# Row factors of the five block boundaries: sums of squares by a matrix of ones, root and reciprocal on 128x320

## The chip, the cores and the metric

The kernel runs on one core of a Trainium2 chip. What counts is the device time of one execution in microseconds, as the median of several runs. The profile is of one execution by itself, with its own time.

## The reference

A recurrent decoder trunk of two layers is computed in f32 for 320 tokens (256 of a new sequence, 64 of eight short continuations), with a model width of 1024:

```python
for l in range(DEPTH):                                   # 2
    h = swiglu(rmsnorm(x, ffn1_norm_pre[l]), ffn1_w_up[l], ffn1_w_down[l])
    x = x + 0.5 * rmsnorm(h, ffn1_norm_post[l])
    h, cb, rh, S = mixer(rmsnorm(x, mix_norm_pre[l]), ...)
    x = x + rmsnorm(h, mix_norm_post[l])
    h = swiglu(rmsnorm(x, ffn2_norm_pre[l]), ffn2_w_up[l], ffn2_w_down[l])
    x = x + 0.5 * rmsnorm(h, ffn2_norm_post[l])
y = rmsnorm(x, final_norm)

def rmsnorm(x, g):
    return x * rsqrt(mean(x * x, axis=-1, keepdims=True) + EPS) * g
```

The mixer has an input projection, a short convolution, a gated linear recurrence, a gated delta rule in chunks and an output projection. Outputs are y and the states.

## The kernel before

Everything is held with channels on the 128 partitions and the 320 tokens along the row: x is eight tiles of 128x320 (k = 0 to 7), and so is hp, the output of the block that just ended. Each weight tile of 128x1024 comes by DMA (`raw`), is rounded on ScalarE (`wh`, L129), and its remainder is taken on VectorE (`wl`, L134). Activations are split in the same way into `xh` and `xl`. A weight unit is then 24 products on TensorE (L157): eight channels by wh with xh, wl with xh, wh with xl, each with 320 columns.

The stream of such units is a `Fill` object `F`: `F(n)` issues the next n products, `F.inter(4, 1)` one channel step of four units at once (12 products), `F.warm(12)` twelve dummy products that keep TensorE going. TensorE's order is the order in which the code is written; the other engines' order is made by a scheduler from priorities, and `tc.high_priority` moves an instruction ahead. Accumulators are PSUM tiles in three rings: mm (3), sm (4) and st (1).

Between two blocks stands `boundary` (L402). There are five: into the mixer (first and fourth, near 235 and 859 us of the span), into the second feed-forward block (second and fifth, near 416 and 1041 us) and into the next layer's first one (third, near 638 us). Each needs two factors per token, that is two times a sum of squares over 1024 channels, a root and a reciprocal:

- The first factor scales hp before it is added to x. The squares of the block's output are added up on VectorE in `acc`, but for the last tile (`slast`). `sumsq_mm` (L228) multiplies slices of 128 tokens by one column of ones, so that the sums lie with tokens on partitions (128x3). `rstd` (L233) takes root (L235) and reciprocal (L236) there, and `rowbc` (L239) spreads each column over a tile and transposes it on TensorE (L242), so that each token's factor lies on all partitions, in PSUM. Then for each k VectorE multiplies hp by it (`bt`, L422), adds it to x (L423), ScalarE and VectorE split x (L225, L226) and ScalarE squares it (L426), and `F.inter` runs the step of the first four units of the next block.
- The second factor is that of the next norm. It isn't applied to x but to the results of the products: it is put into `rsb2` (128x320 in SBUF, L437), and the consumers of each unit multiply by it (L496, L498 in a feed-forward block; L705, L706 for the mixer's eight scalar columns, L667, L668 for its convolution columns). `F(10)` issues ten products while root and reciprocal run.

Two tables set how many products stand between the steps. `ahead` is 8 for feed-forward blocks and 0 for mixers: so many products stand ahead of the second sums. `FL[0]` is the number of products ahead of the transposes of the mixer's scalar projection (L753 in `Mixer.run`), which wait for L705 and L706. `side` holds small work that TensorE does in a boundary: transposes of states (L601) in mixers, of outputs (L1246, L1255) in the second and fifth.

Of the kernel before, what the change touches and what calls it, by code (L numbers as in the profile page):

```python
# [11 lines left out]
AF = mybir.ActivationFunctionType  # L12
# [3 lines left out]
D = 1024  # L16
# [4 lines left out]
T = NP + NB * SL  # L21
# [34 lines left out]
PS = [(0, 1, 2), (0, 2, 1), (0, 2, 1)]  # L56
PO = [0, 0, -1, 0, 1, 1, -1, 2, 2, -1, 2, 1, -1]
XC = []
FL = [14, 37, 32, 9, 15, 8, 0, 14, 0, 11, 10, 4, 0, 11, 5, 0, 11, 12, 14, 6, 0, 11, 16]
FZ = [11, 11, 11, 22, 8, 17]  # L60
FY = [10, 10, 5, 3, 11, 6]

# [1 line left out]
def bc(ap, n):  # L64
    return ap.to_broadcast([ap.shape[0], n])
# [15 lines left out]
def trunk(ctx, tc, x_prompt, x_sample, state_conv, state_rglru, state_delta,  # L81
# [6 lines left out]
    act, dve, pe, pool = nc.scalar.activation, nc.vector, nc.tensor, nc.gpsimd  # L88
# [18 lines left out]
    def smtile():  # L107
        return smp.tile([128, 512], F32, name="sm")
# [7 lines left out]
    def sttile():  # L116
        return stp.tile([128, 512], F32, name="st")
# [87 lines left out]
    ones = consts.tile([128, 128], F32, name="ones")  # L205
    eps_t = consts.tile([128, 1], F32, name="eps_t")
    x = consts.tile([128, KD, T], F32, name="x")
    hp = consts.tile([128, KD, T], F32, name="hp")
    xh = consts.tile([128, KD, T], F32R, name="xh")
    xl = consts.tile([128, KD, T], F32R, name="xl")  # L210
    acc = consts.tile([128, T], F32, name="acc")
    rsb2 = consts.tile([128, T], F32, name="rsb2")
# [7 lines left out]
    def sqtile():  # L220
        return tmp.tile([128, T], F32, name="sq", bufs=3)

    def split_x(k, g):
        h = hv(xh[:, k])
        act(h, pr(x[:, k]), AF.Copy, scale=g)  # L225
        stt(hv(xl[:, k]), pr(x[:, k]), g, h.bitcast(F32), op0=OP.mult, op1=OP.subtract)  # L226

    def sumsq_mm(ps, s, start, stop):  # L228
        for t, (a, b) in enumerate(TOK):
            pe.matmul(ps[:, t:t + 1], s[:, a:b], ones[:, 0:1], start=start and t == 0, stop=stop,  # L230
                      skip_group_check=True)

    def rstd(ps, eps=None):  # L233
        rs = tmp.tile([128, 3], F32, name="rs")
        act(rs, ps[:, 0:3], AF.Sqrt, scale=1.0 / D, bias=eps_t if eps is None else eps)  # L235
        dve.reciprocal(rs, rs)  # L236
        return rs

    def rowbc(rs):  # L239
        rb = smtile()  # L240
        for t, (a, b) in enumerate(TOK):
            pe.transpose(rb[:, a:b], bc(rs[:, t:t + 1], 128), ident)  # L242
        return rb

    sq_first = {}

    def accum(i, n, s, eng=None):
        eng = eng or dve
        if i == 0:
            sq_first[0] = s  # L250
        elif i == 1:
            eng.tensor_add(acc, sq_first[0], s)
        elif i < n - 1:
            eng.tensor_add(acc, acc, s)
# [25 lines left out]
    def vcol(nm, i):  # L280
        return C["vec"][:, 0, rows[nm] + i:rows[nm] + i + 1]
# [119 lines left out]
    def boundary(slast, gname, l, F, n, side, ahead=0):  # L401
        side = list(side) + [None] * 3  # L402
        cnt[0] = -1
        if side[0]:
            side[0]()
        st = sttile()
        sumsq_mm(st, acc, True, False)
        sumsq_mm(st, slast, False, True)
        if side[1]:
            side[1]()  # L410
        with tc.high_priority(offset=HPB):
            rs = rstd(st)
        rb = rowbc(rs)
        if side[2]:
            side[2]()
        F.warm(12)
        st2 = sttile()
        for k in range(KD):
            if k != 1:
                t = tmp.tile([128, T], F32, name="bt")  # L420
            with tc.high_priority(offset=HPB):
                dve.tensor_mul(t, hp[:, k], rb[:, :T])  # L422
                dve.tensor_add(x[:, k], x[:, k], t)  # L423
                split_x(k, vcol(gname, 8 * l + k))
            s = sqtile()
            act(s, x[:, k], AF.Square)  # L426
            accum(k, KD, s, pool if AP else dve)
            F.inter(n, 1)
        F.i = n
        F(ahead)  # L430
        sumsq_mm(st2, acc, True, False)
        sumsq_mm(st2, s, False, True)
        with tc.high_priority(offset=HPB):
            rs = rstd(st2)
        F(10)
        rb2 = rowbc(rs)
        act(rsb2, rb2[:, :T], AF.Copy)  # L437

    def xtoken():
        z = tmp.tile([128, 1], F32, name="tk", bufs=6)  # L440
# [168 lines left out]
    class Mixer:  # L609
# [37 lines left out]
        def mt(self, shape, name, bufs=1, dt=F32):  # L647
            return self.mp.tile(shape, dt, name=name, bufs=bufs)
# [88 lines left out]
        def run(self):  # L737
# [11 lines left out]
            F.inter_done(4, 2)  # L749
            F(FL[0])  # L750
            tp = smtile()
# [32 lines left out]

            F(FL[1])
            self.late_state()
            F(FL[2])
            gp = smtile()
# [16 lines left out]
            qg = mt([128, NH, 192], "qg")  # L805
            F(FL[3])
            grs = []
# [34 lines left out]
            def tok(u0, src, srcs, dst, scl, sums=None):  # L842
                n = 4 if u0 < 8 else 2
                ps = smtile()
                for i in range(n):
                    if u0 < 8:
                        a = src[:, i, 32 * u0:32 * u0 + 128]
                    else:
                        a = srcs[:, 2 * i:2 * i + 2]
                    pe.transpose(ps[:, i * 128:(i + 1) * 128], a, ident)  # L850
                if sums is not None:
                    with tc.high_priority(offset=HPO):
                        for i in range(n):
                            act(dst[:, u0 + i], ps[:, i * 128:(i + 1) * 128], AF.Square,
                                accum_out=sums[:, u0 + i:u0 + i + 1])
                for i in range(n):
                    u = u0 + i
                    act(dst[:, u], ps[:, i * 128:(i + 1) * 128], AF.Copy, scale=scl[:, u:u + 1])
# [3 lines left out]

            F(FL[4])
            for u0 in (0, 4, 8):
                tok(u0, ka, kas, kd, eKD, ss)
                F(FL[5])
            with tc.high_priority(offset=HPO):
# [412 lines left out]
    F = ph.F  # L1280
# [117 lines left out]
    rs = rstd(ss)  # L1398
    rb2 = smtile()
# [16 lines left out]
    for l in range(DEPTH):  # L1416
        side = state_prep(l)
        mids = [(14, side[0])]
        if l == 0:
            mids = [(4 + i, consts_a) for i in range(12)] + [(18, consts_b), (22, side[0])]  # L1420
        s = ph.run(mids)
        mx = Mixer(l, side)
        boundary(s, "mpre", l, mx.F, mx.n, [None, side[2]])
        s = mx.run()
        ph = ffn2(l)
        boundary(s, "f2pre", l, ph.F, ph.n, mx.outputs(ph.fp), 8)
        if l + 1 < DEPTH:
            nxt_side = None
            s = ph.run()
            ph = ffn1(l + 1)  # L1430
            boundary(s, "f1pre", l + 1, ph.F, ph.n, [], 8)
        else:
            ph.run_last()
# [32 lines left out]
```

## Time and profile before

| | |
|---|---|
| median of 3 runs | 1289.98 us (1288.92 to 1290.28) |
| the profiled execution | 1285.95 us, span 1284.2 us |
| TensorE busy with matmuls | 1250.6 us, 97% of the span |
| TensorE busy with weight loads | 1216.2 us, 95% |
| VectorE | 854.0 us, 66% |
| ScalarE | 699.4 us, 54% |
| the chain that ended last | TensorE 89%, VectorE 4%, ScalarE 3% |
| granted clock of TensorE over the span | 0.982 |

A line of a group names the line of the code, the engine, the operation and its tiles. A matmul of f32 tiles shows as two records, a product of rounded tiles as one. Matmuls are pipelined, so that the time from one start to the next is what one costs in a stream, and not its duration.

### The profile page before, as it was taken

The numbers are of one execution on the slowest core, as the hardware profiler recorded it, in microseconds if no ns is written. First come the engines' busy times: TensorE is split into PE (matmuls) and PEld (weight loads), VectorE is DVE, ScalarE is ACT, GpSimd is POOL, SyncE is SP. The second block draws the span as 40 slices with busy tenths as digits, with TensorE's granted clock in tenths as the row PEclk, the third lists the DMA queues.
The fourth block names the chain that finished last, engine by engine and source line by source line (L and its number), as shares of the span: only waits on it lengthen the run. The fifth ranks groups of instructions, "written<-read, shape, count | busy, mean of one in ns | idle before, by whom it ended". The sixth has DMA issues, their size and how long they took to land.

```text
span 1284.2 us, 24470 instructions
## 1 busy us (share of the span) xinstructions
PE 1250.6 (97%) x9812; PEld 1216.2 (95%) x9812; DVE 854.0 (66%) x1536; ACT 699.4 (54%) x1223; POOL 111.9 (9%) x242
## 2 busy tenths in 40 slices
PE   8999999999999999999999999999998999999995
PEld 7999999989879999999999999999897899999995
DVE  4976644799686866654586665459995777666433
ACT  5654444584686644444464444446658675444443
POOL 1100000233120100000000000012321110000001
PEclk8999999999989999999999999999999899999997
DMA  8555555553346455555635555575332646555541
GB/s 211 156 172 159 156 160 161 144 144 90 94 122 177 114 162 164 165 151 162 190 108 163 164 164 152 159 194 132 83 89 70 180 142 177 161 160 155 148 136 42
DMA packets 356102, 187.26 MB, mean 146 GB/s; under 512 B 8986, under 2 KB 353388, under 8 KB 355988
## 3 DMA queue, kind: packets, MB, share of 16 engines
q1 hardware_dynamic: 352980, 178.25, 49.3%
q0 software_dynamic: 2672, 6.65, 1.9%
q8 instruction: 77, 1.26, 0.4%
q10 hardware_dynamic: 336, 0.79, 0.2%
q14 instruction: 37, 0.30, 0.1%
HBM read 179.16 MB, written 6.51 MB: 145 GB/s over the span
## 4 chain that ended last, share of the span: by engine, by line
PE 89%; DVE 4%; ACT 3%; DMA 1%; SPq 1%; issue 1%; POOL 1%; ACTq 0%; DVEq 0%
PE mm L157 43%; PE sm L157 38%; PE sm L907 2%; PE st L230 1%; PE sm L1194 1%; PE sm L971 1%; DMA xtok<-in_x_sample_dram 1%; ACT wh L129 0%; ACT hp L1072 0%; DMA raw<-in_ffn_w_up_dram 0%; DVE xr L1097 0%; ACT vo L1078 0%; POOL sv L869 0%; ACT hp L1079 0%; DVE DN L821 0%
## 5 line engine op out<-in xcount | busy, mean ns | idle before, releaser
L134 DVE TENSOR_TENSOR wl<-raw,wh 128x1024 fp32r<-128x1024 f32 x321 | 384.5, 1198 | 214.0 <-ACT wh L129 209.8
L129 ACT ACTIVATE wh<-raw 128x1024 fp32r<-128x1024 f32 (+1 forms) x316 | 326.7, 1035 | 360.4 <-issue 125.4
L157 PE MATMUL mm<-xh,wh 128*128 128x320 f32 x976 | 295.9, 307 | 1.6 <-ACT wh L1332 0.9
L157 PE MATMUL mm<-xh,wl 128*128 128x320 f32 x976 | 293.6, 305 | 0.9 <-DVE wl L134 0.9
L157 PE MATMUL mm<-xl,wh 128*128 128x320 f32 x976 | 287.4, 304 | 0.0
L157 PE MATMUL sm<-xh,wh 128*128 128x320 f32 x720 | 215.6, 299 | 0.0
L157 PE MATMUL sm<-xl,wh 128*128 128x320 f32 x720 | 215.5, 299 | 0.0
L157 PE MATMUL sm<-xh,wl 128*128 128x320 f32 x720 | 215.4, 299 | 0.0
L157 PEld LDWEIGHTS mm<-xh,wh 128*128 128x128 f32 x976 | 187.1, 193 | 7.5 <-issue 3.0
L157 PEld LDWEIGHTS mm<-xh,wl 128*128 128x128 f32 x976 | 185.9, 192 | 3.3 <-DVE wl L134 1.3
L157 PEld LDWEIGHTS mm<-xl,wh 128*128 128x128 f32 x976 | 184.3, 192 | 1.8 <-issue 0.8
L157 PEld LDWEIGHTS sm<-xh,wl 128*128 128x128 f32 x720 | 136.1, 189 | 0.3 <-DVE wl L134 0.3
L157 PEld LDWEIGHTS sm<-xh,wh 128*128 128x128 f32 x720 | 136.1, 189 | 0.0
L157 PEld LDWEIGHTS sm<-xl,wh 128*128 128x128 f32 x720 | 136.1, 189 | 0.0
L157 PE MATMUL sm<-gh,wh 128*128 128x320 f32 x374 | 112.2, 300 | 0.0
L157 PE MATMUL sm<-gh,wl 128*128 128x320 f32 x374 | 111.8, 299 | 0.0
L157 PE MATMUL sm<-gl,wh 128*128 128x320 f32 x374 | 111.8, 299 | 0.0
L157 PE MATMUL mm<-gh,wh 128*128 128x320 f32 x330 | 99.0, 300 | 0.0
L157 PE MATMUL mm<-gh,wl 128*128 128x320 f32 x330 | 98.7, 299 | 0.0
L157 PE MATMUL mm<-gl,wh 128*128 128x320 f32 x330 | 98.7, 299 | 0.0
L157 PEld LDWEIGHTS sm<-gh,wl 128*128 128x128 f32 x374 | 70.7, 189 | 0.0
L157 PEld LDWEIGHTS sm<-gh,wh 128*128 128x128 f32 x374 | 70.7, 189 | 0.0
(438 smaller groups left out, 1969.5 us busy)
## 6 DMA issues: line engine op xcount, KB each, us to landing
raw<-in_ffn_w_up_dram SPq DMA_DIRECT2D x173, 512.0 KB, 3.9
raw<-in_ffn_w_down_dram SPq DMA_DIRECT2D x64, 512.0 KB, 3.9
raw<-in_w_in_dram SPq DMA_DIRECT2D x48, 512.0 KB, 4.1
raw<-in_ffn_w_down_dram SPq DMA_DIRECT2D x32, 384.0 KB, 3.5
raw<-in_w_out_dram SPq DMA_DIRECT2D x16, 512.0 KB, 4.1
aux<-in_state_delta_dram SPq DMA_DIRECT2D x8, 512.0 KB, 7.3
out_dram<-aux POOLq DMA_DIRECT2D x8, 512.0 KB, 5.7
raw<-in_ffn_w_up_dram SPq DMA_DIRECT2D x6, 256.0 KB, 7.3
```

What stands on the lines that cost most here:

```text
L129: act(wh[:, :nk], raw[:, :nk], *((AF.Copy,) if tok is None or tok[0] else (AF.Identity, tok[1]())))
L134: (sub or dve).tensor_sub(wl[:, :nk], raw[:, :nk], wh[:, :nk].bitcast(F32))
L157: pe.matmul(self.blk.ps(), w, il(xx), start=self.first and self.pos == 1, stop=self.last and self.pos == 3 * self.nk)
L230: pe.matmul(ps[:, t:t + 1], s[:, a:b], ones[:, 0:1], start=start and t == 0, stop=stop, skip_group_check=True)
L907: pe.matmul(ps[HF[h], 64 * i:64 * i + 64], lhs(u, h), rhs(u, h), start=True, stop=True)
L971: pe.matmul(ps[32 * j:32 * j + 32, 128 * i:128 * i + 128], kz[:, h, i, c:c + 32], SS[p][:, j // 2, 4 * (j % 2) + b], start=b == 0, stop=b ...
L1194: pe.matmul(ps2[j], kd[r, u], ve[r], start=True, stop=True)
```

## The change

The sums of squares are made with the full 128x128 matrix of ones as the stationary operand and the squares (128x320) as the moving one, so that every partition of the result holds each token's sum. Root and reciprocal then work on 128x320 and write `rsb2`; the transposes go. Both factors of a boundary go through `rsb2`. The ten products ahead of the second transposes go, and `FL[0]` goes from 14 to 18.

```diff
-FL = [14, 37, 32, 9, 15, 8, 0, 14, 0, 11, 10, 4, 0, 11, 5, 0, 11, 12, 14, 6, 0, 11, 16]
+FL = [18, 37, 32, 9, 15, 8, 0, 14, 0, 11, 10, 4, 0, 11, 5, 0, 11, 12, 14, 6, 0, 11, 16]
...
+    pst = []
+
+    def sums(a, b):
+        pst[:] = [sttile()]
+        pe.matmul(pst[0][:, :T], ones, a, start=True, stop=False)
+        pe.matmul(pst[0][:, :T], ones, b, start=False, stop=True)
+
+    def rowfactor():
+        act(rsb2, pst[0][:, :T], AF.Sqrt, scale=1.0 / D, bias=eps_t)
+        dve.reciprocal(rsb2, rsb2)
...
-        st = sttile()
-        sumsq_mm(st, acc, True, False)
-        sumsq_mm(st, slast, False, True)
+        sums(acc, slast)
         if side[1]:
             side[1]()
         with tc.high_priority(offset=HPB):
-            rs = rstd(st)
-        rb = rowbc(rs)
+            rowfactor()
...
         F.warm(12)
-        st2 = sttile()
...
-                dve.tensor_mul(t, hp[:, k], rb[:, :T])
+                dve.tensor_mul(t, hp[:, k], rsb2)
...
-        sumsq_mm(st2, acc, True, False)
-        sumsq_mm(st2, s, False, True)
+        sums(acc, s)
         with tc.high_priority(offset=HPB):
-            rs = rstd(st2)
-        F(10)
-        rb2 = rowbc(rs)
-        act(rsb2, rb2[:, :T], AF.Copy)
+            rowfactor()
```

The scheduler also changes the order on VectorE. In the first boundary, behind the last weight splits of the block that ended, it was this for the first factor (numbers tell buffers apart: bt_2704 is the product of k = 0 and then of k = 1, bt_2745 that of k = 2):

```order
L236 RECIPROCAL rs_2683<-rs_2683 128x3 [waits Activation_49]
L422 TENSOR_TENSOR bt_2704<-hp_82,sm_2686 128x320 [waits PE_49]
L423 TENSOR_TENSOR x_81<-x_81,bt_2704 128x320 [waits DVE_49]
L422 TENSOR_TENSOR bt_2704<-hp_82,sm_2686 128x320 [waits DVE_49]
L422 TENSOR_TENSOR bt_2745<-hp_82,sm_2686 128x320
```

and is now this (bt_2694 is k = 0, bt_2735 is k = 2):

```order
L254 RECIPROCAL rsb2_86<-rsb2_86 128x320 [waits Activation_49]
L429 TENSOR_TENSOR bt_2694<-hp_82,rsb2_86 128x320 [waits DVE_49]
L429 TENSOR_TENSOR bt_2735<-hp_82,rsb2_86 128x320
L430 TENSOR_TENSOR x_81<-x_81,bt_2694 128x320 [waits DVE_49]
L430 TENSOR_TENSOR x_81<-x_81,bt_2735 128x320 [waits DVE_49]
L429 TENSOR_TENSOR bt_2694<-hp_82,rsb2_86 128x320 [waits DVE_49]
```

The product of k = 2 now stands ahead of the sum of k = 0. At the end of the same boundary, for the second factor, VectorE had this row (wl are remainders of weight units of the mixer, PY the scaled scalar columns, cb the convolution's input):

```order
L134 TENSOR_TENSOR wl_2876<-raw_2873,wh_2875 128x1024 [waits DMAHW1_49,Activation_49]
L619 TENSOR_TENSOR wsl_9701<-wsr_9699,wsh_9700 128x64 [waits Activation_49]
L134 TENSOR_TENSOR wl_2884<-raw_2881,wh_2883 128x1024 [waits DMAHW2_49,Activation_49]
L236 RECIPROCAL rs_2870<-rs_2870 128x3 [waits Activation_49]
L134 TENSOR_TENSOR wl_3016<-raw_3013,wh_3015 128x1024 [waits DMAHW3_49,PE_49,Activation_49]
L705 TENSOR_TENSOR PY_2903<-sm_2690,rsb2_86 8x320 [waits Activation_49]
L706 TENSOR_TENSOR PY_2903<-sm_2690,rsb2_86 8x64
L667 TENSOR_TENSOR cb_2906<-mm_2713,rsb2_86 128x256 [waits PE_49]
```

and has this:

```order
L134 TENSOR_TENSOR wl_2907<-raw_2904,wh_2906 128x1024 [waits DMAHW1_49,Activation_49]
L622 TENSOR_TENSOR wsl_9644<-wsr_9642,wsh_9643 128x64 [waits Activation_49]
L134 TENSOR_TENSOR wl_2915<-raw_2912,wh_2914 128x1024 [waits DMAHW2_49,Activation_49]
L134 TENSOR_TENSOR wl_2997<-raw_2994,wh_2996 128x1024 [waits DMAHW3_49,Activation_49]
L254 RECIPROCAL rsb2_86<-rsb2_86 128x320 [waits Activation_49]
L708 TENSOR_TENSOR PY_2859<-sm_2681,rsb2_86 8x320 [waits DVE_49,PE_49]
L709 TENSOR_TENSOR PY_2859<-sm_2681,rsb2_86 8x64
L670 TENSOR_TENSOR cb_2862<-mm_2703,rsb2_86 128x256 [waits PE_49]
```

The third remainder now stands ahead of the reciprocal, and the scaled columns follow right behind the reciprocal, without a transpose in between.

## Rows read from the trace of the kernel before

**Rows 1.** The chain that ended last, in order of time: start, us, what.
```profile
445.43 9.78 PE mm L157 x72
```

**Rows 2.** Timeline of the first boundary's first factor: start us, us, engine, line, operation.
```profile
234.81 0.44 ACT L450 ACTIVATE sq<-sm 128x320 f32<-128x320 f32 x1 [1.38 <-PE sm L157]
...
235.30 0.83 PE L230 MATMUL st<-ones,sq 128*128 128x1 f32 x6
...
236.47 0.18 DVE L236 RECIPROCAL rs<-rs 128x3 f32<-128x3 f32 x1 [1.78 <-ACT rs L235]
...
237.28 0.49 DVE L422 TENSOR_TENSOR bt<-hp,sm 128x320 f32<-128x320 f32 x1 [0.63 <-PE sm L242]
...
238.32 0.59 ACT L225 ACTIVATE xh<-x,vec 128x320 fp32r<-128x320 f32 x1 [1.30 <-DVE x L423]
...
238.97 0.30 PE L157 MATMUL sm<-xh,wsh 128*8 128x320 f32 x1
```

**Rows 3.** VectorE's groups by form: count, busy us, mean ns, idle before.
```profile
L499 DVE TENSOR_TENSOR t<-t,t 128x320 f32<-128x320 f32 x88 | 43.2, 494 | 8.8 <-ACT t L497 1.1
...
L236 DVE RECIPROCAL rs<-rs 128x3 f32<-128x3 f32 x12 | 2.1, 175 | 19.3 <-ACT rs L235 19.1
L766 DVE RECIPROCAL sv<-sv 128x10 f32<-128x10 f32 x2 | 0.4, 216 | 0.0
L266 DVE RECIPROCAL sp<-sp 128x10 f32<-128x10 f32 x2 | 0.4, 206 | 0.0
...
L559 DVE RECIPROCAL sq<-sq 128x1 f32<-128x1 f32 x3 | 0.4, 147 | 0.0
```

**Rows 4.** ScalarE's groups by form: an activation out of PSUM with a bias column.
```profile
L1072 ACT ACTIVATE hp<-sm,vec 128x320 f32<-128x320 f32 x16 | 7.0, 521 | 0.0
```

**Rows 5.** Timeline of the first mixer: f32 matmuls with 320 columns, ten records.
```profile
347.21 2.85 PE L1071 MATMUL sm<-xr,wbd 128*128 128x320 f32 x10
```

**Rows 6.** Timeline of the first boundary, TensorE's second and third channel step.
```profile
242.22 0.30 PE L157 MATMUL sm<-xl,wsh 128*8 128x320 f32 x1 [0.20 <-DVE xl L226]
...
242.77 0.30 PE L157 MATMUL sm<-xh,wsh 128*8 128x320 f32 x1
```

**Rows 7.** Stretches: length, busy PE, PEld, DVE, ACT, POOL, granted clock, DMA share, GB/s.
```profile
281.40:284.80 3.40, 1.02 (x16) 0.83 (x14) 2.28 (x10) 2.73 (x5) 1.50 (x4) 1.00 0.09 25
284.80:288.20 3.40, 3.40 (x20) 3.28 (x17) 3.31 (x11) 3.03 (x9) 0.00 (x0) 0.50 0.02 5
32.78:34.21 1.43, 0.00 (x0) 0.03 (x1) 1.15 (x2) 1.05 (x3) 0.00 (x0) 1.00 1.10 283
34.21:38.00 3.79, 3.79 (x27) 3.55 (x28) 2.64 (x8) 2.55 (x4) 0.78 (x2) 1.00 1.18 282
```

**Rows 8.** Timeline of the second boundary's second factor.
```profile
434.90 0.72 PE L230 MATMUL st<-ones,acc 128*128 128x1 f32 x6
...
436.16 0.38 PE L157 MATMUL sm<-xl,wh 128*128 128x320 f32 x1
...
437.60 0.49 PE L242 MATMUL sm<-ident,rs 128*128 128x128 f32 x3
...
438.07 0.30 PE L157 MATMUL sm<-xh,wl 128*128 128x320 f32 x1
...
438.65 0.49 DVE L496 TENSOR_TENSOR t<-mm,rsb 128x320 f32<-128x320 f32 x1 [0.72 <-ACT rsb L437]
...
440.26 1.22 DVE L134 TENSOR_TENSOR wl<-raw,wh 128x1024 fp32r<-128x1024 f32 x1
```

**Rows 9.** Timeline of the first boundary's second factor, ahead of the mixer.
```profile
252.55 0.72 PE L230 MATMUL st<-ones,acc 128*128 128x1 f32 x6
...
253.58 1.23 DVE L134 TENSOR_TENSOR wl<-raw,wh 128x1024 fp32r<-128x1024 f32 x1 [0.72 <-ACT wh L129]
...
256.77 0.20 DVE L706 TENSOR_TENSOR PY<-sm,rsb 8x64 f32<-8x64 f32 x1
...
257.57 0.35 PE L753 MATMUL sm<-ident,PY 8*128 8x8 f32 x3
```

## The prediction

> **What bounds the kernel now.** I read the chain of work that ended last first. In the long stretches it is TensorE alone: 72 products of the weight loops in 9.78 us [rows 1], 0.136 us each, without a gap. So an edit in VectorE or ScalarE counts only where TensorE waits for them. The change touches the five boundaries between blocks (near 235, 416, 638, 859 and 1041 us of the span), and each has two such places.
>
> The first place is the row factor of the block that just ended. In the first boundary the last square is ready at 234.81 + 0.44 = 235.25 us; then come, one behind the other, the sums on TensorE (235.30, 0.83 us), a tiny root and a 0.18 us reciprocal on 128x3 (236.47), three transposes, the first product on VectorE at 237.28, the sum, the split into xh at 238.32, and the first real product of TensorE at 238.97 [rows 2]: 3.72 us in which TensorE does only dummy products and small transposes. The second place is the factor of the next norm. There TensorE has weight products to do, so it loses only what its own queue holds: in the feed-forward boundaries from 434.90 to 436.16 for the sums and from 437.60 to 438.07 around the transposes [rows 8]. In the two mixers three transposes of the scalar projection follow at 257.57 [rows 9], and they need the factor's consumers.
>
> **The unknown: a reciprocal on 128x320.** The trace has none that wide, but it has the operation at 1, 3 and 10 elements a partition: 147, 175, 206 and (another line) 216 ns [rows 3]. It grows with width. A plain VectorE operation on 128x320 takes 494 ns [rows 3], so about 0.49 us is the lower end. The flattest of the measured slopes is (206 - 175) / 7 = 4.4 ns an element, which gives 0.175 + 317 x 4.4 ns = 1.57 us; from 1 to the dearer 10 it is (216 - 147) / 9 = 7.7 ns, which gives 2.6 us. I take 2.1 us, the middle of the two slopes, since nothing in the rows favours one of them; 0.49 to 2.6 us stay as ends.
>
> The Trainium skill (VectorE: DVE Perf Modes, First, the fixed hardware budget) says that the reciprocal runs as a hardware iterative divide with a repeat count of 8, which speaks against making it wide. With the 0.96 GHz of that page an estimate is 320 x 8 / 0.96 = 2.67 us and a start of some 0.15, together 2.8; the sum below would then be 4.9 us higher, 1309.3. The trace agrees that width costs, at a somewhat lower slope, 4.4 to 7.7 ns.
>
> **A. First factor, five times.** The sums become two f32 matmuls of 128x320. Such matmuls took 2.85 us for ten records, two to a matmul [rows 5], so 0.57 us a matmul; the one on the last square would end near 236.0 instead of 236.13, and the other is done before. The root on 128x320 out of PSUM with a bias column is like the 521 ns activation [rows 4]: 236.04 to 236.56. The reciprocal runs 236.60 to 238.70. The transposes and their two handovers go, which took 237.28 - 236.65 = 0.63 us [rows 2]. VectorE's order also moves: the product of k = 2 now stands ahead of the sum of k = 0, some 0.4 us. So product at 238.72, sum near 239.5, xh near 240.06, and 0.65 us behind it, as now, TensorE at 240.7: 1.74 us later. Of this a part comes back: now the low half of k = 1 is late and TensorE reaches k = 2 only at 242.77 [rows 6], though 24 products of 0.136 from 238.97 would end at 242.23; that 0.54 us can be caught while the start is late anyway. Between 1.20 and 1.74 I take 1.35 us, and the same for the other four, whose steps are the same: +6.8 us. Each 0.1 us of reciprocal is worth 0.5 us here.
>
> **B. The clock.** TensorE now does its dummies at once, as nothing ahead of them waits for the factor, and then stands. Sums issued by 235.85, small transposes to 236.4, twelve dummies to 238.1: an idle 2.5 us until 240.7 in mixer boundaries one and four, some 3 us in the third, which has no transposes there, and 1.5 us in the other two, where output transposes fill more. In the trace of before a stretch in which TensorE was busy for 1.02 of 3.40 us was followed by one with a granted clock of 0.50, 1.2 instead of 2.4 GHz, for 3.4 us; after an idle 1.43 us the clock stayed at 1.00 [rows 7]. So three first factors, and the two mixer stalls under D (2.6 us idle), are long enough to lose the clock. 3.4 us at half speed cost 1.7 us where TensorE is the bound, and about 1.2 us at the first factor, where it waits 0.5 us anyway: all five would be 3 x 1.2 + 2 x 1.7 = 7.0 us. Not every fall need come; I take +5.0 us, with 0 and 7 as ends.
>
> **C. Second factor, three feed-forward boundaries.** The sums took 1.26 us of TensorE (434.90 to 436.16) and take four records, 1.1 us; the transposes took 438.07 - 437.60 less one product, 0.33 us, and go [rows 8]. Together -0.5 each, -1.5 us. The wide root and reciprocal lie beside the weight products: TensorE has 64 of them, 8.7 us, before it needs an accumulator that the first consumer (438.65) frees, and the next low weight half (440.26 to 441.48) is not due until then, near 444.8; both come some 1 to 2 us later. Were the cover gone, each would cost that much.
>
> **D. Second factor, two mixers.** Here it is on the path. The three low-half splits now stand ahead of the reciprocal on VectorE: the second runs from 253.58 for 1.23 us [rows 9], the third behind it to 256.05, the reciprocal to 258.15, and the two scalar products, 0.4 and 0.2 us, to 258.8. TensorE meanwhile has only 18 products (24 and the transposes before), is done at 253.6 + 2.45 = 256.1, and waits 2.6 us for the scalar transposes: 258.82 instead of 257.57. Six products that stood ahead are still to do, 0.82 us. Together +2.05 each, +4.1 us; queued behind the reciprocal on VectorE are all convolution copies, so the chain behind it is not ahead to make this good. With a reciprocal of 0.49 us it would be +0.4 each.
>
> **The sum.** 6.8 + 5.0 - 1.5 + 4.1 = +14.4 us on the profiled execution's 1285.95 us, so 1300.4. The median of the runs, 1289.98 us, is 4.0 higher, so 1304.4.
>
> **Rivals.** (1) The cost in width is only a fill that is over after a few elements, and 128x320 costs about 0.54 us. For it: the rise from 3 to 10 is less than from 1 to 3 in ns an element. Against it: it still rises, and a plain fill would show at width 1. Then A is 1.35 - 1.56 = -0.2 each, the idle times stay under 1 us so B is 0, C stays, D is 2 x 0.5: -1.0 - 1.5 + 1.0 = -1.5 us, 1288.5, no change. The point from which it decides: seven waits on the path (five A, two D) against 1.5 us saved, break-even near 0.75 us, 1.9 ns an element. (2) The reciprocal is slow but the clock holds: B is 0, 1299.4. For it: the idle stretches are hardly longer than those that lost the clock, and 12 dummies stand right ahead. (3) VectorE becomes the bound behind the boundaries: 2.1 us more of it, where it also has the splits and the gate products of every unit, makes the next weight halves late, about 2 us at each of three feed-forward blocks: 1310.4. Against it: 3.3 us of slack at 441.48.
>
> **How the numbers follow.** Forecast 0.60, rival 1 0.10, rival 2 0.20, rival 3 0.10. Low end: reciprocal 1.57 (seven times 0.53 less, -3.7) and no fall (-5.0) is +5.7, 1295.7; high end: 2.6 (+3.5) and all falls (+2.0) is +19.9, 1309.9. The scheduler's reordering of the mixers' ScalarE and VectorE queues, unpriced, adds 2 to 3 on either side: 1293.5 to 1313. Outside lie rival 1 and some of the tails. Slower by over 0.2% (2.6 us, about what a measurement here can tell from none) holds for all but rival 1 and a tail: 0.88; within 0.2% 0.08; faster 0.04.
>
> **What would show it.** The width of the reciprocal's ten rows, 2.1 us or 0.5, decides most. The first real product should come 1.7 us later against the last square. The clock should read 0.50 right behind the boundaries. In the mixers the scalar transposes should show an idle wait on VectorE of over 2 us; in feed-forward blocks TensorE should run through. Wrong would be: reciprocals under 0.8 us, or a delay that a mixer's later waits swallow.

## The result: 1.8% slower, and the profile of the changed kernel

| | before | after |
|---|---|---|
| median of 4 runs | 1289.54 us | 1312.39 us |
| lowest and highest | 1288.92 to 1290.28 | 1311.10 to 1315.14 |
| ratio after / before | | 1.0179, 95% interval 1.0164 to 1.0194 |
| profiled execution | 1285.95 us | 1311.10 us |
| its span | 1284.2 us | 1309.4 us |

The time lies in the forecast range (1293.5 to 1313) at its upper end, 8 us above the forecast 1304.4. The sign and the price of the reciprocal were right; where the 8 us come from is the question of the experiments. The profiled run of before took 3.6 us less than the median of its runs, so what is read from the two traces adds up to 25.15 us, where the medians differ by 22.85.

VectorE's group by line, with lowest, median and highest duration in ns, answers [rows 3]:

```profile
L254 DVE RECIPROCAL rsb<-rsb x10: 2145/2150/2153, 237.0 to 1087.0; 128x320 f32<-128x320 f32 x10
```

The first boundary's first factor, by engine (start us, us, engine, line, operation, idle before and who ended it), answers [rows 2]:

```profile
234.95 0.70 PE L249 MATMUL st<-acc,ones 128*128 128x320 f32 x2
235.64 0.81 PE L250 MATMUL st<-sq,ones 128*128 128x320 f32 x2
...
236.98 1.80 PE L197 MATMUL sm<-xh,wsh 128*8 128x320 f32 x12
241.78 0.30 PE L157 MATMUL sm<-xh,wsh 128*8 128x320 f32 x1 [3.01 <-ACT xh L225]
...
236.49 0.53 ACT L253 ACTIVATE rsb<-st,eps_t 128x320 f32<-128x320 f32 x1 [0.48 <-PE st L250]
...
237.04 2.15 DVE L254 RECIPROCAL rsb<-rsb 128x320 f32<-128x320 f32 x1 [2.02 <-ACT rsb L253]
239.23 1.47 DVE L429 TENSOR_TENSOR bt<-hp,rsb 128x320 f32<-128x320 f32 x2
240.63 1.41 DVE L430 TENSOR_TENSOR x<-x,bt 128x320 f32<-128x320 f32 x2
```

Sums, root, reciprocal stand one behind the other as forecast, and TensorE stands still for 3.01 us ahead of its first real product. Two things were not forecast: the pairs on L429 and L430 take 1.47 and 1.41 us, though one such operation takes 0.49 [rows 2, 3] and a pair 0.89 in the third boundary (below), and nothing is caught up later (table below).

The second factor ahead of the first mixer, VectorE and then TensorE, answers [rows 9]:

```profile
256.42 2.36 DVE L134 TENSOR_TENSOR wl<-raw,wh 128x1024 fp32r<-128x1024 f32 x2 [0.72 <-ACT wh L129]
258.70 2.15 DVE L254 RECIPROCAL rsb<-rsb 128x320 f32<-128x320 f32 x1
...
261.53 0.32 PE L756 MATMUL sm<-ident,PY 8*128 8x8 f32 x3 [2.45 <-issue]
```

And the second factor in the second boundary, answers [rows 8]: TensorE runs through it, and VectorE's reciprocal lies beside weight products.

```profile
446.75 0.70 PE L249 MATMUL st<-acc,ones 128*128 128x320 f32 x2
...
448.82 2.15 DVE L254 RECIPROCAL rsb<-rsb 128x320 f32<-128x320 f32 x1
```

Start times of TensorE's marks in the two traces, and what each stage added (a fall of the clock is a stretch at 1.2 GHz, 3.4 us or longer in these traces; "(clock)" marks the one in this table):

| mark on TensorE | before | after | later by | added since the mark above |
|---|---|---|---|---|
| first boundary, sums | 234.61 | 234.95 | 0.34 | |
| first real product | 238.97 | 241.78 | 2.81 | +2.5 (first factor) |
| second sums | 252.55 | 255.40 | 2.85 | 0 |
| scalar transposes of the mixer | 257.57 | 261.53 | 3.96 | +1.1 (second factor) |
| second boundary, sums | 416.16 | 426.47 | 10.31 | **+6.35 (rest of the mixer)** |
| first real product | 420.69 | 432.47 | 11.78 | +1.5 |
| second sums | 434.90 | 446.75 | 11.85 | +0.1 |
| third boundary, sums | 637.61 | 648.86 | 11.25 | -0.6 (second factor, feed-forward) |
| first real product | 641.96 | 655.11 | 13.15 | +1.9 |
| second sums | 656.36 | 671.01 | 14.65 | +1.5 (clock) |
| fourth boundary, sums | 859.06 | 873.12 | 14.06 | -0.6 |
| first real product | 863.42 | 879.92 | 16.50 | +2.4 |
| scalar transposes | 882.02 | 899.61 | 17.59 | +1.1 |
| fifth boundary, sums | 1040.72 | 1064.69 | 23.97 | **+6.4** |
| first real product | 1045.24 | 1070.69 | 25.45 | +1.5 |
| end of the span | 1284.24 | 1309.39 | 25.15 | -0.3 |

Of 25 us nearly 13 arise inside the two mixers, behind the scalar transposes, in code that the change doesn't touch. It is not the clock: over these stretches, 257.57 to 416.16 and 882.02 to 1040.72 us before, 261.53 to 426.47 and 899.61 to 1064.69 after, the mean granted clock is 0.96 in all four. Where TensorE waits there is seen in its waits of over 0.8 us in the first mixer, behind the scalar transposes; before, then after:

```profile
284.57 0.54 PE L890 MATMUL sm<-ka 128*64 128x64 f32 x8 [2.38 <-DVE nA L914]
351.14 1.88 PE L1071 MATMUL sm<-xr,wbd 128*128 128x320 f32 x6 [1.08 <-ACT hp L1072]
370.27 2.07 PE L1194 MATMUL sm<-nA,kd 32*128 32x512 f32 x2 [2.14 <-DVE qa L1158]
```

```profile
288.85 2.08 PE L888 MATMUL sm<-ka 128*128 128x128 f32 x8 [3.85 <-DVE nA L917]
360.02 1.88 PE L1074 MATMUL sm<-xr,wbd 128*128 128x320 f32 x6 [2.17 <-ACT hp L1075]
380.84 2.07 PE L1197 MATMUL sm<-nA,kd 32*128 32x512 f32 x2 [3.63 <-DVE tok L725]
```

The three waits last 5.60 us before and 9.65 after, 4.05 of the 6.35; two shorter ones that before doesn't have, 0.76 and 0.52 us, are 1.3 more. The first of the three is told by ScalarE's queue, and by what it feeds. Before, then after: squares of kd, the load of an activation table, and the addition that needs all ten squares. A power on GpSimd (2.25 and 2.00 us) and then nA, which TensorE waits for, follow on it:

```profile
279.56 0.30 ACT L854 ACTIVATE kd<-sm 128x128 f32<-128x128 f32 x1
...
281.00 1.28 ACT L700 ACT_TABLE_LOAD   x1
...
279.98 0.17 DVE L868 TENSOR_SCALAR sv<-sv 128x10 f32<-128x10 f32 x1
```

```profile
282.64 1.28 ACT L703 ACT_TABLE_LOAD   x1
...
284.51 0.27 ACT L857 ACTIVATE kd<-sm 128x128 f32<-128x128 f32 x1
...
284.90 0.17 DVE L871 TENSOR_SCALAR sv<-sv 128x10 f32<-128x10 f32 x1 [1.11 <-ACT kd L857]
```

Before, the tenth square starts at 279.56 and the table load stands behind all ten. After, eight squares run, then the load of 1.28 us, an activation, and only then the last two, the tenth at 284.51. The scheduler has put ScalarE's instructions in another order. The other two waits lead back to the queues in the same way. Before, then after: what ScalarE runs ahead of the hp that the second wait ends on, and when VectorE reaches the qa that the third wait ends on:

```profile
349.40 1.28 ACT L1056 ACTIVATE qa<-qa,fs 128x128 f32<-128x128 f32 x4 [0.91 <-POOL fs L1051]
...
369.81 0.41 DVE L1158 TENSOR_TENSOR qa<-sm,kso 128x256 f32<-128x256 f32 x1
```

```profile
356.44 1.28 ACT L1081 ACT_TABLE_LOAD   x1
...
358.29 1.26 ACT L1059 ACTIVATE qa<-qa,fs 128x128 f32<-128x128 f32 x4
...
379.26 1.19 DVE L134 TENSOR_TENSOR wl<-raw,wh 128x1024 fp32r<-128x1024 f32 x1
380.38 0.41 DVE L1161 TENSOR_TENSOR qa<-sm,kso 128x256 f32<-128x256 f32 x1
```

After, a table load and one activation stand ahead of qa and hp on ScalarE (before, that load stands behind them, at 353.61), and a weight remainder stands ahead of the other qa on VectorE (before, the next one comes behind it, at 370.93). The trace names tok, which starts right behind qa, as the end of the third wait after; qa ends 0.05 us ahead of TensorE's start in both traces. Both traces have 31 table loads: none was added, they moved.

The clock behind the first and the third boundary (length, busy PE, PEld, DVE, ACT, POOL, granted clock, DMA share, GB/s), answers [rows 7]:

```profile
238.78:241.78 3.00, 0.00 (x0) 0.00 (x0) 2.96 (x5) 0.58 (x1) 2.91 (x7) 1.00 1.10 248
241.80:245.20 3.40, 3.08 (x21) 2.54 (x22) 3.40 (x9) 2.42 (x6) 0.00 (x0) 1.00 0.04 9
...
656.50:659.90 3.40, 3.40 (x15) 3.40 (x14) 3.40 (x10) 1.92 (x5) 0.00 (x0) 0.51 0.00 0
```

TensorE idled 3.00 us in the first and kept 2.4 GHz; behind the third it ran at 1.2 GHz for 3.4 us. Of the five falls that the prediction counted, three at first factors and two at the mixers' new stalls, this profile has one. (Its other falls lie inside the mixers.)

### The profile page after: what moved, and what is told of

Same layout as the page of the kernel before. It is cut to its first block, busy times and chain, and to the rows that moved or that the text cites. A ratio compares the mean times of both kernels' runs of the same rounds, so it can differ in the third digit from the quotient of the medians.

```text
span 1309.4 us, 24249 instructions
## 1 busy us (share of the span) xinstructions
PE 1247.6 (95%) x9702; PEld 1206.4 (92%) x9702; DVE 872.2 (67%) x1536; ACT 699.1 (53%) x1218; POOL 116.2 (9%) x242
## 3 DMA queue, kind: packets, MB, share of 16 engines
q8 instruction: 76, 1.25, 0.4%
## 4 chain that ended last, share of the span: by engine, by line
PE 84%; DVE 7%; ACT 5%; issue 2%; DMA 1%; POOL 0%; ACTq 0%; DVEq 0%
PE mm L157 41%; PE sm L157 36%; PE sm L910 2%; DVE wl L134 1%; DVE rsb L254 1%; ACT wh L129 1%; DMA raw<-in_ffn_w_up_dram 1%; PE sm L1197 1%; PE sm L974 1%; ACT hp L1075 1%; DVE xr L1100 0%; DVE bt L429 0%; DMA xtok<-in_x_sample_dram 0%; ACT kd L857 0%; PE st L250 0%
## 5 line engine op out<-in xcount | busy, mean ns | idle before, releaser
L157 PE MATMUL mm<-xh,wh 128*128 128x320 f32 x976 | 295.7, 308 | 6.9 <-ACT xh L225 6.8
L157 PE MATMUL mm<-xh,wl 128*128 128x320 f32 x976 | 294.1, 306 | 0.8 <-DVE wl L134 0.4
L157 PE MATMUL mm<-xl,wh 128*128 128x320 f32 x976 | 287.0, 304 | 0.0
L157 PE MATMUL sm<-xl,wh 128*128 128x320 f32 x720 | 216.0, 300 | 0.0
L157 PE MATMUL sm<-xh,wl 128*128 128x320 f32 x720 | 215.4, 299 | 0.0
L157 PE MATMUL sm<-xh,wh 128*128 128x320 f32 x720 | 215.4, 299 | 0.0
L157 PEld LDWEIGHTS mm<-xh,wh 128*128 128x128 f32 x976 | 187.0, 193 | 13.1 <-ACT xh L225 7.5
L157 PEld LDWEIGHTS mm<-xh,wl 128*128 128x128 f32 x976 | 186.1, 192 | 3.7 <-DVE wl L134 1.8
L157 PEld LDWEIGHTS mm<-xl,wh 128*128 128x128 f32 x976 | 184.0, 192 | 1.9 <-issue 0.8
L157 PEld LDWEIGHTS sm<-xh,wl 128*128 128x128 f32 x720 | 136.1, 189 | 0.3 <-DVE wl L134 0.3
L157 PEld LDWEIGHTS sm<-xh,wh 128*128 128x128 f32 x720 | 136.1, 189 | 0.2
L157 PEld LDWEIGHTS sm<-xl,wh 128*128 128x128 f32 x720 | 136.1, 189 | 0.2
L157 PE MATMUL sm<-gh,wh 128*128 128x320 f32 x374 | 112.2, 300 | 0.0
L157 PE MATMUL sm<-gh,wl 128*128 128x320 f32 x374 | 111.8, 299 | 0.0
L157 PE MATMUL sm<-gl,wh 128*128 128x320 f32 x374 | 111.8, 299 | 0.0
L157 PE MATMUL mm<-gh,wh 128*128 128x320 f32 x330 | 99.0, 300 | 0.0
L157 PE MATMUL mm<-gh,wl 128*128 128x320 f32 x330 | 98.7, 299 | 0.0
L157 PE MATMUL mm<-gl,wh 128*128 128x320 f32 x330 | 98.7, 299 | 0.0
L157 PEld LDWEIGHTS sm<-gh,wl 128*128 128x128 f32 x374 | 70.7, 189 | 0.0
L157 PEld LDWEIGHTS sm<-gh,wh 128*128 128x128 f32 x374 | 70.7, 189 | 0.0
```

Of the source, the lines that this page charges most:

```text
L157: pe.matmul(self.blk.ps(), w, il(xx), start=self.first and self.pos == 1, stop=self.last and self.pos == 3 * self.nk)
```

## Experiments

The theory at the start: the change is three separate things, worth by the traces +11.3 us (first factor with its clock), -1.8 (second factor, feed-forward) and +14.9 (second factor, mixers), and the third is dear because with fewer weight products ahead of the scalar transposes the scheduler reorders ScalarE's and VectorE's queues. The rival: the mixers lose by 2.15 us more of VectorE and the late factor, whatever the order. Times in us below are the ratio less one, times 1289.5; the changed kernel is +23.1 in this measure. Runs of before spread from 1285.8 to 1291.1, so a difference of 2 us rests on the interval and not on two runs. Numbers "by the marks" are differences to the one trace of before, which lies near the lower end of that spread, and come out higher: up to the first boundary's sums, ahead of every edit, the other traces lie between 0.5 us earlier and 2.2 us later than it.

### The parts alone

```diff
 # e1_first_only: kernel before, in boundary()
+        sums(acc, slast)
         with tc.high_priority(offset=HPB):
-            rs = rstd(st)
-        rb = rowbc(rs)
+            rowfactor()
...
-                dve.tensor_mul(t, hp[:, k], rb[:, :T])
+                dve.tensor_mul(t, hp[:, k], rsb2)
```

> The kernel before with the wide sums, root and reciprocal in the first factor of the five boundaries alone; the second factors are as before. By the prediction's terms A and B (three of the five falls of the clock) it is 5 x 1.35 + 3 x 1.2 = +10.4 us, +6.8 if the clock holds. By the trace of the changed kernel, where the first real product comes 2.5, 1.5, 1.9, 2.45 and 1.45 us later against its own sums and one fall of the clock costs some 1.5, it is +11.3. If instead what was gained and lost in the mixers comes from the first factor's delay (their queues reordered because of it), it is +20 or more.

Measured: 1300.09 us, ratio 1.0086 (1.0061 to 1.0111), +11.1. The +20 of a delay that upsets the mixers is out; the three waits in the first mixer are 2.38, 1.08 and 2.14 us as before. Its profile has three falls of the clock outside the mixers, behind the third, fourth and fifth boundary, where the changed kernel's has the third alone:

```profile
649.10:652.50 3.40, 3.40 (x14) 3.40 (x14) 3.40 (x10) 1.91 (x5) 0.00 (x0) 0.50 0.00 0
...
874.40:877.80 3.40, 3.40 (x15) 2.95 (x15) 3.40 (x9) 1.89 (x4) 0.00 (x0) 0.50 0.00 0
...
1058.70:1062.10 3.40, 3.40 (x14) 3.40 (x14) 3.40 (x9) 2.48 (x6) 1.02 (x2) 0.50 0.15 38
```

```diff
 # e2_mixer_second_only: kernel before; e7_ffn_second_only: the same with gname != "mpre", FL unchanged
-FL = [14, 37, ...
+FL = [18, 37, ...
...
         F(ahead)
+        if gname == "mpre":
+            sums(acc, s)
+            with tc.high_priority(offset=HPB):
+                rowfactor()
+            return
         sumsq_mm(st2, acc, True, False)
```

> The kernel before with the wide second factor in the two mixers alone, and 18 weight products ahead of the scalar transposes in place of 10 + 14. By the prediction's term D it is +4.1 us (+7.5 with a fall of the clock in each). By the trace of the changed kernel, where each mixer loses 7.45 us from its second sums to the sums of the next boundary, it is +14.9. If the mixers lose only together with the delayed first factor, it is about +4.

Measured: 1301.92 us, ratio 1.0105 (1.0086 to 1.0125), +13.5. So the mixers' second factor alone costs three times the forecast term, without a first factor that is late. Its profile has a fall of the clock at the scalar transposes of both mixers (granted clock 0.51 from 259.8 to 266.7 and from 894.6 to 898.1 us), as the prediction's term B had it; the changed kernel's profile has neither.

> The kernel before with the wide second factor in the three feed-forward boundaries alone. By the prediction's term C it is -1.5 us; by the changed kernel's trace, where each of these places comes out 0.6 us earlier, -1.8 (1287 us, about 0.9986 of before). By the prediction's rival 3, weight halves late behind the boundaries, it is slower, up to +6.

Measured: 1287.89 us, ratio 0.9986 (0.9978 to 0.9995), -1.8. Term C holds, and rival 3 of the prediction is out. The three parts add up: 11.1 + 13.5 - 1.8 = 22.8, against 23.1 for the whole; as each of the first two is known to 2.5 to 3 us, so close an agreement is partly chance.

### What the mixers lose by

```diff
 # e3_cheap_for_reciprocal: changed kernel
-        dve.reciprocal(rsb2, rsb2)
+        dve.tensor_scalar(rsb2, rsb2, 1.0, None, op0=OP.mult)
```

> The changed kernel with a multiplication by 1.0 on 128x320 in place of each reciprocal (the factor is then the root and not its inverse), so that the operation takes some 0.5 us and not 2.15; in the mixers the instructions of every engine stand in the order of the changed kernel. If the duration of the reciprocal is what costs, in the mixers too, it is rival 1 of the prediction: 1288.5 us, no change. If the mixers lose by the new order of ScalarE's and VectorE's queues and by the missing six products, they still lose some 5 of their 7.45 us each, and it is 1288.5 + 10 = 1298 or more.

Measured: 1294.47 us, ratio 1.0045 (1.0029 to 1.0060), +5.8: between the two, above 1288.5 by 6 and below 1298 by 3.5. It is not the duration alone, and not the order alone. By the marks the first factors cost between -0.3 and +0.1 each and the mixers 4.6 and 5.2 us, as was expected of them; of the 4 us between these 9.8 and the +5.8, the trace of before lies 3.0 below the median of the runs beside e3, and e3's trace 1.5 above the median of its own. The waits of TensorE in the mixers are the changed kernel's to a hundredth, with no wide reciprocal in the program:

```profile
286.46 1.16 PE L888 MATMUL sm<-ka 128*128 128x128 f32 x8 [3.85 <-DVE nA L917]
356.56 1.88 PE L1074 MATMUL sm<-xr,wbd 128*128 128x320 f32 x6 [2.17 <-ACT hp L1075]
377.39 2.07 PE L1197 MATMUL sm<-nA,kd 32*128 32x512 f32 x2 [3.63 <-DVE tok L725]
```

```diff
 # e4_spare_reciprocal_in_mixers: kernel before
             rs = rstd(st2)
+            if gname == "mpre":
+                dve.reciprocal(acc, acc)
```

> The kernel before, with one reciprocal on 128x320 more at the second factor of the two mixers, in place on acc, whose values have been used by then; it stands right ahead of the reciprocal on 128x3. Everything else stands as before but for a few weight splits and convolution copies that trade places. If 2.15 us of VectorE at this place is what costs the mixers their 7.45 us each, whatever the order, it is +10 to +15. If the order does it, it is the wait for the factor alone, 2.15 us less the cover of ten products: +1 to +2 each, +2 to +4.

Measured: 1290.80 us, ratio 1.0015 (1.0005 to 1.0026), +1.9. 2.15 us more of VectorE, with the order of before, cost one microsecond a mixer. The rival falls, with one limit: this reciprocal starts at 254.32 us with a weight remainder still behind it, where the changed kernel's starts at 258.70 behind both. What the later place costs is seen in e6 below.

```diff
 # e5_before_18_products: kernel before
-FL = [14, 37, ...
+FL = [8, 37, ...
 # e6_after_24_products: changed kernel
-FL = [18, 37, ...
+FL = [24, 37, ...
```

> The kernel before with 8 in place of 14 weight products ahead of the scalar transposes of each mixer, so 10 + 8 = 18 as in the changed kernel; no wide operation anywhere. ScalarE's queue in the mixers then has the changed kernel's order (eight squares of kd in a row, a table load between the eighth and the ninth). If the number of products ahead, through the order that the scheduler then makes, is what costs the mixers, each loses some 4.6 to 5.2 us, as with the cheap operation in place of the reciprocal: +9 to +10, 1298 to 1299. If the order is harmless by itself and the wide factor is needed for the loss, it is within 1.6 us of before (six products of 0.136 us less ahead, twice).

Measured: 1296.38 us, ratio 1.0051 (1.0035 to 1.0068), +6.6; expected were +9 to +10 or under 1.6. By the marks the mixers lose 5.9 and 4.2 us, 10.1 together, against the same trace of before. One number in a table, with nothing wide in the program, gives the mixers the changed kernel's waits:

```profile
285.25 2.08 PE L885 MATMUL sm<-ka 128*128 128x128 f32 x8 [3.84 <-DVE nA L914]
356.63 1.88 PE L1071 MATMUL sm<-xr,wbd 128*128 128x320 f32 x6 [2.17 <-ACT hp L1072]
377.45 2.07 PE L1194 MATMUL sm<-nA,kd 32*128 32x512 f32 x2 [3.64 <-DVE tok L722]
```

> The changed kernel with 24 in place of 18 products ahead of the scalar transposes; ScalarE's queue in the mixers has the order of the kernel before again. If the order costs 4.6 to 5.2 us in each mixer: 1312.4 - 10 = 1302.5 us, and each mixer loses 2.3 to 2.9 us against before, not 7.45, with the three long waits of TensorE in it back near 2.38, 1.08 and 2.14 us. If the wide reciprocal makes the loss and the order does nothing, it stays within 1.6 us of 1312.4.

Measured: 1305.44 us, ratio 1.0121 (1.0103 to 1.0138), +15.6, that is 7.5 less than the changed kernel, where 10 less were expected. The waits are those of before again, and two shorter ones stand at the scalar transposes:

```profile
262.70 0.32 PE L756 MATMUL sm<-ident,PY 8*128 8x8 f32 x3 [1.64 <-issue]
263.88 0.37 PE L157 MATMUL mm<-xh,wh 128*128 128x320 f32 x1 [0.86 <-DVE sv L765]
290.56 0.45 PE L893 MATMUL sm<-ka 128*64 128x64 f32 x8 [2.38 <-DVE nA L917]
356.27 1.88 PE L1074 MATMUL sm<-xr,wbd 128*128 128x320 f32 x6 [1.08 <-ACT hp L1075]
375.39 2.07 PE L1197 MATMUL sm<-nA,kd 32*128 32x512 f32 x2 [2.14 <-DVE qa L1161]
```

From both sides the order is worth 6.6 to 7.5 us by the medians (8.4 to 10.1 by the marks), and what is left of the mixers' 13.5, some 6 to 7, is the wide factor itself. All kernels with 18 products ahead whose mixers were read (the changed one, e2, e3, e5) have the table load ahead of hp and the remainder ahead of qa, with waits of 2.17 and 3.6 us; all with 24 (before, e1, e4, e6) have neither, with 1.08 and 2.14. By the marks of its trace, from the second sums to the next boundary's sums, the mixers lose 2.6 and 3.9 us, where those of the changed kernel lose 7.45 each; its second mixer runs at a granted clock of 0.95, the first at 0.96. The wait of 0.86 us falls on the first product of a new unit (L157 into mm); the trace names sv on VectorE as what ended it. By its place it waits for an accumulator that VectorE's convolution copies free, which are queued behind the reciprocal; that is argued, and was not tried by itself.

### The slow pairs in the mixers' boundaries

In the third boundary, where GpSimd does nothing, the same pairs of the changed kernel take 0.89 us each; in the first, GpSimd copies run beside them (after's trace, VectorE in the third boundary, then GpSimd in the first):

```profile
653.14 0.89 DVE L429 TENSOR_TENSOR bt<-hp,rsb 128x320 f32<-128x320 f32 x2
653.95 0.89 DVE L430 TENSOR_TENSOR x<-x,bt 128x320 f32<-128x320 f32 x2
```

```profile
240.01 0.76 POOL L669 COPY cb<-stT 128x24 f32<-128x24 f32 x3
240.72 0.98 POOL L898 COPY Nt<-identc 128x640 f32<-128x640 f32 x1
```

```diff
 # e8_gpsimd_quiet: changed kernel (e9: the same two edits on e7's kernel)
-            pool.tensor_copy(cs[:, :, 0:3], self.stT[:, ct]...)
+            if 8 <= ct < 11:
+                act(cs[:, :, 0:3], self.stT[:, ct]..., AF.Copy)
+            else:
+                pool.tensor_copy(cs[:, :, 0:3], self.stT[:, ct]...)
...
-            pool.tensor_copy(Nt, ...)
+            act(Nt, ..., AF.Copy)
```

> The changed kernel with four GpSimd copies of each mixer's beginning (three of cb from stT, one of Nt from identc) on ScalarE, which is idle there; they now run beside the first products and sums of VectorE in the boundary ahead of the mixer. Everything else stands in the same order. If they are why these two pairs take 1.47 and 1.41 us in that boundary and 0.89 each in the feed-forward boundaries, the pairs take 0.89 here too, and from the end of the reciprocal to TensorE's first real product it is some 1.1 us less. If the pairs wait for something else (the sums' buffers, the block output), they stay at 1.4.

Measured: a single run of 1311.89 us, too close to the changed kernel to be told from it; the trace tells:

```profile
237.22 2.15 DVE L254 RECIPROCAL rsb<-rsb 128x320 f32<-128x320 f32 x1 [2.06 <-ACT rsb L253]
239.41 0.89 DVE L429 TENSOR_TENSOR bt<-hp,rsb 128x320 f32<-128x320 f32 x2
240.22 0.89 DVE L430 TENSOR_TENSOR x<-x,bt 128x320 f32<-128x320 f32 x2
...
241.38 0.44 PE L157 MATMUL sm<-xh,wsh 128*8 128x320 f32 x1 [2.47 <-ACT xh L225]
```

The pairs are back at 0.89. From the end of the reciprocal to TensorE's first real product it is 241.38 - 239.37 = 2.01 us, against 241.78 - 239.19 = 2.59: 0.58 less, half of the 1.1 expected. All of it is the pair of products: from the start of the sums to TensorE it is 1.16 us here and 1.15 in the changed kernel, so what the second sum lost was not on that path. GpSimd's copies slow VectorE's operations on two tensors. The Trainium skill (GPSIMD Engine Reference, 2. Architecture) says that GpSimd's read and write port into SBUF are shared with VectorE; the trace agrees, with 0.89 against 1.47 us.

> The kernel before with the wide second factor in the three feed-forward boundaries, as before this (-1.8 us), and with the four GpSimd copies ahead of each mixer on ScalarE. In the trace of before TensorE reaches the third block's products at 242.77 and could at 242.23, while VectorE's two splits into xl take 1.82 us beside these copies, and 0.55 each elsewhere. If the copies are why, each mixer's boundary is 0.5 to 0.6 us shorter: -2.8 to -3.0 in all, 1286.8, about 0.9978 of before. If ScalarE's 1.2 us of copies comes into the way instead (ahead of the root), it is -1.8 or less.

Measured: 1286.07 us, ratio 0.9984 (0.9972 to 0.9995), -2.1, where -2.8 to -3.0 were expected. It is faster than both kernels, but from e7 (0.9986) the intervals can't tell it. By the marks each mixer's boundary is 0.36 us shorter than before, and not 0.5 to 0.6. In its trace the splits that took 1.82 us in the kernel before take 1.01:

```profile
240.25 1.01 DVE L226 SCALAR_TENSOR_TENSOR xl<-x,vec,xh 128x320 fp32r<-128x320 f32 x2
```

### The clock

```diff
 # e10_after_24_dummies: changed kernel
-        F.warm(12)
+        F.warm(24)
```

> The changed kernel with 24 in place of 12 dummy products behind each first factor: 1.63 us more in which TensorE is busy while it waits, so that it idles 1.4 us, and not 3.0, ahead of the first real product in the mixers' boundaries and the second feed-forward one, and about 0.2, not 1.8, in the two others. All else stands as in the changed kernel. If the falls of the clock behind the first factors cost what they cost in the trace with the wide first factor alone (three falls, 1.2 to 1.7 us each), they are gone and it is 1.5 to 4.4 us faster than the changed kernel, 1308 to 1311 us, and the profile has no granted clock of 0.50 within 10 us of a boundary. If such falls cost nothing, because TensorE waits there anyway, it is the same as the changed kernel, 1312.4.

Measured: 1313.67 us, ratio 1.0196 (1.0180 to 1.0211), +25.3, the same as the changed kernel within the intervals. The falls at the boundaries are gone, as expected; but both mixers lose the clock at their scalar transposes instead, where the changed kernel had the same idle 2.45 and 2.40 us and kept it:

```profile
263.80:267.20 3.40, 3.40 (x14) 3.40 (x14) 3.10 (x17) 2.48 (x6) 0.73 (x4) 0.50 1.16 290
902.10:905.50 3.40, 3.40 (x14) 3.40 (x14) 3.39 (x19) 1.84 (x5) 0.96 (x5) 0.50 1.16 286
```

A fall does cost: from its sums to its second sums the third boundary loses 1.8 us here and 3.4 in the changed kernel, where it has one; and the mixers, which now have one more each, at the transposes, lose 9.9 and 9.0 us in place of 7.45. But which of several like stalls loses the clock is not settled by the length of that stall alone, and filling five of them won nothing. Why the falls moved stays open. Nor are they the wide factor's alone: in e4, e7 and e9, whose first factors are those of before, the clock falls in the third boundary too (granted 0.51 for 3.4 us; in e7 from 642.9 us, where TensorE had idled 0.56 us, at a cost of 1.15). The trace of before has no such fall (granted 1.00 from 637.6 to 656.3 us).

## Why the prediction was right, and where it was short

**The reciprocal: right.** 2.15 us against 2.1, between the slopes of the narrow rows; from 10 elements to 320 it is (2150 - 206) / 310 = 6.3 ns an element. The Trainium skill (VectorE: DVE Perf Modes, First, the fixed hardware budget) gives a repeat count of 8, and the estimate from it, 2.8 us, was 0.65 too long; that width costs, the trace confirms.

**A, first factor, forecast +6.8: too small; by the trace it is +9.8.** It is 2.5, 1.5, 1.9, 2.4 and 1.5 us. Two steps failed. The 0.39 to 0.54 us that were to be caught up didn't come: the second sums are as late as the first real product (2.85 and 2.81). And one price was taken for all five, from operations without a neighbour: the two mixers' boundaries have GpSimd copies beside VectorE, +0.58 (e8), the third comes out near the 1.74 without catching up, and the two with output transposes less.

**B, the clock, forecast +5.0: not a fixed number.** The changed kernel's profile has one fall of the five, +1.5; with the wide first factor alone there were three, 1.5 + 1.2 + 1.7 = 4.4 by the same marks; e6, with the same first factors, has three (first, third and fourth boundary); filling the stalls moved them. That an idle time like the one of [rows 7] decides is the step that failed: 3.01 us kept the clock and 0.56 us (e7) lost it. For the first factors the forecast of A and B together is 6.8 + 3.6 x 5 / 7 = 9.4 (the 5.0 taken were 5/7 of the 7.0 for all falls); measured are +11.1 (e1), 1.7 more. Rival 2, a clock that holds, was closer to this one profile than the forecast was.

**C, feed-forward second factor, forecast -1.5: right.** -0.6 each by the marks, -1.8 as measured alone. The cover named (weight products) hid the reciprocal.

**D, mixers' second factor, forecast +4.1 (6.5 with its two falls of the clock): the term that was mis-sized, +13.5.** What it worked out was right: the scalar transposes come 1.1 us later, where 1.25 were forecast, behind a stall of 2.45 us, where 2.6 were. The step that failed is "queued behind the reciprocal on VectorE are all convolution copies, so the chain behind it is not ahead to make this good": it took the rest of the mixer as it was, later by a constant. Two numbers are missing in it. The order of ScalarE's and VectorE's queues, which the prediction called "unpriced" and gave 2 to 3 us on either side, is worth 6.6 to 7.5 us and only on one side; it comes from 18 products ahead in place of 24, and not from the factor (e5 has it without the factor, e6 has the factor without it). And the wide factor with the old order costs 2.6 to 3.9 us a mixer; with 24 products ahead the forecast's own sum, 2.05 less the six products' 0.82, is 1.2. Of the 2.6, 1.1 arise at the scalar transposes and 0.86 at the unit behind them; the rest stays open. The new order could be seen before any run, like VectorE's in the section on the change: a table load between the eighth and ninth square of kd. One such load is 1.28 us in the trace of before.

**The sum.** By measured parts 11.1 - 1.8 + 13.5 = 22.8; the forecast had 9.4 - 1.5 + 6.5 (D with its two stalls' share of B, 3.4 x 5 / 7 = 2.4) = 14.4. Of the 8.4 between them 7.0 are D and 1.7 the first factors, with -0.3 from C. That the time still lies in the range is partly luck: its upper end was made of a reciprocal of 2.6 us and all five falls, which this profile does not show (2.15 us and one fall), and the queues' order, priced at 2 to 3 us, filled that room.

## What to carry to other kernels

A change that alters how many independent products stand ahead of a wait can also alter what the scheduler does behind it, as here; where the new order puts an activation table load or a weight remainder into a chain, price it and the chain, whatever the change was about. Replacing a reciprocal on 128x3 and three transposes by one on 128x320 pays only where weight products cover it: here in the feed-forward boundaries (-0.6 us each), not at a factor that TensorE waits for (+1.5 to +2.5 each). Move one part at a time: of three edits one gained, and alone it makes a kernel faster than before, by 0.14%. And a profile is one run: where it lies among its kernel's runs (here 3.6 us below the median) goes into every difference that is read from it.

## What the runs showed of the hardware that was not expected

- VectorE's operations on two tensors take 1.5 times as long and more beside small GpSimd copies: a pair 1.47 in place of 0.89 us (e8). Whether GpSimd's copies lose by it too is not shown: the copy of 128x640 takes 0.98 us beside the sums on L430 and 0.71 beside the splits of the kernel before, and no trace has it alone.
- TensorE kept 2.4 GHz after an idle 3.01 us in one boundary and lost it after 3.12 in another of the same run; stalls of 2.45 and 2.40 us kept it in the changed kernel and lost it in e10, and in e7 it fell behind an idle 0.56. A forecast of single falls from the idle time is not to be had from these rows; the cost of one fall behind a first factor is, 1.2 to 1.7 us.
- A reciprocal on VectorE costs 6.3 ns for each element of width between 10 and 320, the same at every place where the wide one ran (2145 to 2153 ns, ten times).
